# Second block's head projections: pinned high parts, earlier rotary tables, oldest places first

## The chip, the cores and the metric

One core of a Trainium2 chip runs the whole kernel. The metric is device time in microseconds (us) of one execution, median of three runs. TensorE is called PE in the profile, VectorE DVE, ScalarE ACT, GpSimd POOL, SyncE SP. Times of the trace are us from the start of the span.

## The reference

A decoder trunk of one layer over 2048 tokens of width 1024: retention and pooling mixers with one output projection, cross-attention into 256 memory tokens, a gated MLP with a causal convolution, a last norm. The part that the change touches is the combined input projection and what makes its columns into queries, keys, gates and pooled groups:

```
q = rope(q.reshape(B, S, H, Dh), positions)
k = rope(k.reshape(B, S, H, Dh), positions) * (Dh ** -0.5)
...
return jnp.concatenate([t1 * cos - t2 * sin, t2 * cos + t1 * sin], axis=-1)
```

Everything is float32.

## The kernel before, in words

The tokens are worked in two blocks of 1024. A product of two float32 matrices is made of three matmuls on rounded numbers: each operand is split into a high part (rounded, ScalarE) and a low part (what the rounding left, VectorE), and `passes` (lines 268 to 270) runs high by high, high by low and low by high. `split` makes both parts; for weights `Member.high` (L1118) and `low` (L242) do.

The second block's projections stand in `head_projections`. Eight pairs of column tiles (PAIRS) are each computed from seven products of sums of quarters instead of eight plain ones: 56 `items` in all, each of twelve matmuls (4 row tiles, 3 passes). For an item three things are needed.

- Its weight: `fetch` (L1112, SyncE) loads 256 KB from the weights (`w_qkgu`) or from sums of weights that POOL's DMAs made earlier (`Ad`), into one of seven places (`raws`: halves of R, and two of S).
- The weight's high and low part: `fill` takes one of four pairs (`prs`: three in Q, one in another S), calls `high`, and on the next call `low`, which frees the place.
- Its right-hand side, `operand`: sums of quarters of the block's input, split into G and E. `quarter_sums` makes two sets while the values run on TensorE. It leaves two more sums in four slots of Z; `turned_sums` splits them into the values' old place (`split` for the first four tiles, `negated`, L1596, for the others), then Z has room.

`scaled_tables` asks SyncE for the rotary tables (`rope_d`, L1631: four transfers of 64 partitions, 256 KB each, cosine and sine) into the first freed Z slots, and VectorE multiplies them by the row norms. They are needed when a pair of queries or keys is finished (`final`). Both generators are run from `todo`, two `step`s after each item.

The scheduler of the framework may move instructions on an engine; `tc.keep_in_program_order` keeps one where the program has it, `tc.issue_after` puts what is in it behind an instruction. Under the projections POOL goes on making sums of the MLP's weights (`Ud`): a small ScalarE instruction (halo, L1031) starts each burst of DMAs. After the last item the output projection begins: its first weights (L1978, L1991, L1992) are loaded to halves of R and S that the items leave, split by L258. `settle` splits the finished heads (L258, G and E).

Of the kernel before, what the change touches and what calls it, by code (L numbers as in the profile page):

```python
# [11 lines left out]
AF = mybir.ActivationFunctionType  # L12
# [5 lines left out]
KT = D // P  # L18
SEQ = 2048
NMEM = 256  # L20
T = 1024
SUB = 512
# [114 lines left out]
def trunk(ctx, tc, xT, memT, pos, w_qkgu, w_v, wkv, wqT, wo, wout_r, wout_p, poolT, w_up, w_dn, vecs, consts, outT):  # L137
    nc = tc.nc
    pe, act, dve, pool, sp = nc.tensor, nc.scalar, nc.vector, nc.gpsimd, nc.sync
# [17 lines left out]
    def new_s(dtype, at):  # L157
        return cp.tile([P, T], dtype, tag=f"S{at}", name=nm("S"))
# [8 lines left out]
    R = cp.tile([P, 3 * T], F32, tag="R", name="R")  # L167
    Q = cp.tile([P, 3 * T], F32R, tag="Q", name="Q")
    S = [new_s(F32, j) for j in range(2)]
    raws = Places([(R, j * T) for j in range(3)] + [(r, 0) for r in S], T)  # L170
# [70 lines left out]
    def tt(eng, out, a, b, op):  # L241
        return eng.tensor_tensor(out=out, in0=a, in1=b, op=op)  # L242
# [6 lines left out]
    def stt(out, a, s, b, op0=ALU.mult, op1=ALU.add):  # L249
        dve.scalar_tensor_tensor(out=out, in0=a, scalar=s, in1=b, op0=op0, op1=op1)  # L250
# [4 lines left out]
    def split(src, hi, lo, g=None, kept=False):  # L255

        if g is None:
            one = act.activation(hi, src, AF.Copy)  # L258
            tt(dve, lo, src, hi.bitcast(F32), ALU.subtract)
        else:  # L260
            one = act.activation(hi, src, AF.Identity, scale=g)
            stt(lo, src, g, hi.bitcast(F32), ALU.mult, ALU.subtract)
        if kept:
            tc.keep_in_program_order(one)
# [36 lines left out]
    def xpair(k, s):  # L301
        return X[:, 2 * k, s * SUB : (s + 1) * SUB], X[:, 2 * k + 1, s * SUB : (s + 1) * SUB]
# [796 lines left out]
    class Member:  # L1099
# [15 lines left out]
        def high(self, i, pr):  # L1115
            w = self.n * P
            p2 = pr.r.rearrange("p (i n) -> p i n", i=2)
            act.activation(p2[:, 0, :w], self.raw[i].f[:, :w], AF.Copy)  # L1118
            return p2[:, 0, :w], p2[:, 1, :w]
# [436 lines left out]
    def fourth(r, j):  # L1556
        return r.r[:, 2 * j * SUB : (2 * j + 1) * SUB], r.r[:, (2 * j + 1) * SUB : (2 * j + 2) * SUB]

    def part_of(z, i, j):
        at = (j // 2) * 2 * T + i * T + (j % 2) * SUB  # L1560
        return z.f[:, at : at + SUB]

    def quarter_sums(b, t1, t2, z):
# [11 lines left out]
        for j in range(KT // 2):  # L1575
            x11, x12, x21, x22 = ahead.pop(0)
            d3, d4 = part_of(z, 0, j), part_of(z, 1, j)
            g1, g2 = mixg[:, j : j + 1], mixg[:, j + 4 : j + 5]
            r = TT.take()
            t = r.f[:, :SUB]  # L1580
            tc.keep_in_program_order(act.activation(t, x12, AF.Identity, scale=g1))
            tc.keep_in_program_order(tt(dve, x12, x11, x12, ALU.subtract))
            split(x12, *fourth(t1, j), g1)
            yield
            stt(d3, x22, g2, t, ALU.mult, ALU.subtract)
            stt(x11, x11, g1, d3, ALU.mult, ALU.add)
            negated(x11, *fourth(t2, j))
            yield
            stt(d4, x21, g2, x11, ALU.mult, ALU.subtract)
            r.free()  # L1590
            if j + 2 < KT // 2:
                ahead.append(load(j + 2))
            yield

    def negated(src, hi, lo):
        act.activation(hi, src, AF.Copy, scale=-1.0)  # L1596
        stt(lo, src, -1.0, hi.bitcast(F32), ALU.mult, ALU.subtract)

    def head_projections(b, v, rb, t1, t2, z):
# [2 lines left out]
        nonlocal raws, prs  # L1602
        pieces, far = B.arenas[0], new_e(F32)
        more = new_s(F32R, 0)
        raws = Places([(R, j * SUB) for j in range(5)] + [(S[1], j * SUB) for j in range(2)], SUB)
        side = Arena(R, 5 * SUB, 1, SUB).take().f
        prs = Places([(Q, j * T) for j in range(3)] + [(more, 0)], T)
        t3 = pieces.take(4)
        todo, ready, mix, gates, outs, tables = [], [], [None] * KT, {}, {}, []

        def place():
            return Z.take() if Z.room() else far.take()

        def turned_sums():
            for j in range(KT // 2):
                split(part_of(z, 0, j), *fourth(t3, j))
                yield
            z.free(0, 1)
            z.free(2, 1)
            for j in range(KT // 2):  # L1620
                negated(part_of(z, 1, j), *xpair(j, 1))
                yield
            z.free(1, 1)
            z.free(3, 1)

        def scaled_tables():
            out = Z.take(2)
            tables.append(out)
            for to, half in ((0, 0), (0, 1), (2, 0), (1, 1)):
                p, i = slice(64 * half, 64 * half + 64), min(to, 1)  # L1630
                sp.dma_start(out.f[p, i * T : (i + 1) * T].rearrange("p (s c) -> p s c", s=NS), rope_d[to].rearrange("(s p) c -> p s c", s=NS))  # L1631
            yield
            yield
            for i in range(2):
                for s in range(NS):
                    d = out.f[:, i * T + s * SUB : i * T + (s + 1) * SUB]
                    tt(dve, d, d, rb[s].f[:, :SUB], ALU.mult)
                yield
# [37 lines left out]
        class Heads(Member):  # L1676
# [6 lines left out]
            def begun(self):  # L1683
                both_gates = self.groups[0] // 4 == 2
                self.acc = []
                for n in self.groups:
                    if n // 4 == 2:
                        gates[n % 4] = None if both_gates else [TT.take() for _ in range(NS)]
                    if n // 4 == 2 and not both_gates:
                        self.acc.append([g.f[:, :SUB] for g in gates[n % 4]])  # L1690
                    else:
                        r = place()
                        self.acc.append([r.f[:, q * SUB : (q + 1) * SUB] for q in range(NS)])
                        outs[n] = r

            def evac(self, i, ps):
                role, q = ((0, 0), (1, 1), (0, 1), (0, 0), (1, 1), (0, 1), (1, 0))[i]
                d = self.acc[role][q]
                if (role, q) == (1, 0):
                    self.final(role, q, d, ps)  # L1700
                elif (role, q) in self.seen:
                    tt(dve, d, d, ps, ALU.subtract if role else ALU.add)
                    self.final(role, q, d, d)
                else:
                    self.seen.add((role, q))
                    act.activation(d, ps, AF.Copy, scale=-1.0 if role else 1.0)
# [85 lines left out]
        def step():  # L1792
            if todo and next(todo[0], True) is not None:
                todo.pop(0)

        todo += [turned_sums(), scaled_tables()]
        for at, (m, i) in enumerate(items):
            while len(made) <= at or highs:
                fill()
# [3 lines left out]
            pr = made[at].r.rearrange("p (i n) -> p i n", i=2)  # L1803
# [29 lines left out]
        raws = Places([(R, j * T) for j in range(3)] + [(r, 0) for r in S], T)  # L1833
# [72 lines left out]
    todo = folded_weights()  # L1906
# [16 lines left out]
    for b in range(NB):  # L1923
# [19 lines left out]
        else:  # L1943
            t1, t2 = (B.arenas[0].take(4) for _ in range(2))
            v, z = Z.take(4), Z.take(4)
# [11 lines left out]
            finish()  # L1957
            rb = normed[1]
            mix = head_projections(b, v, rb, t1, t2, z)
        for r in rb:  # L1960
            r.free()
# [129 lines left out]
    raws = Places([(R, j * SUB) for j in range(6)] + [(r, j * SUB) for r in S for j in range(2)], SUB)  # L2091
# [114 lines left out]
```

## Time and profile before

| | |
|---|---|
| median of 3 runs | 2466.07 us (2465.82 to 2468.02) |
| profiled execution | 2467.87 us, of it span 2466.1 us |
| PE busy | 2417.9 us, 98% |
| weight loads on PE busy | 2019.7 us, 82% |
| DVE busy | 1726.2 us, 70% |
| ACT busy | 1288.9 us, 52% |
| POOL busy | 316.1 us, 13% |
| mean granted clock of PE | 0.992 |

A row of a timeline reads: start, length, engine, line, operation, output tile <- input tiles, form, and in brackets how long the engine had been idle before it and what ended that. The busy share says little here, since PE is nearly always busy; what a stage may still give shows in PE's pauses and in the granted clock of the stretches around them. The values of the second block end and its head projections begin near 701 us; the output projection follows near 895 us.

### The profile page before, as it was taken

The page shows a single profiled execution, that of the slowest core. Times are in us where ns is not written, and L with a number is a line of the kernel's source. Part 1 is how long each engine was busy: PE and PEld are TensorE (multiplying, and loading weights), DVE is VectorE, ACT ScalarE, POOL GpSimd, SP SyncE. Part 2 cuts the span into 40 slices and gives each one's busy share as a digit, 9 for nine tenths or more (in the row PEclk, how much of TensorE's full clock was granted, in tenths as well). Part 3 has the DMA queues.
Part 4 walks back from the last instruction along what each step waited for, and adds up shares of the span by engine and source line. Part 5 has one row for each costly group of instructions (what it writes and reads, how often), then busy time and mean ns, then how long its engine had stood idle before and what let it go on. Part 6 is the DMA issues. An engine that isn't in the chain of part 4 may idle for free.

```text
span 2466.1 us, 33272 instructions
## 1 busy us (share of the span) xinstructions
PE 2417.9 (98%) x11294; PEld 2019.7 (82%) x11294; DVE 1726.2 (70%) x2917; ACT 1288.9 (52%) x2349; POOL 316.1 (13%) x485
## 2 busy tenths in 40 slices
PE   6999999999989999999999999999999999999997
PEld 6888888888878887878888888888888888888886
DVE  8646576564756665565778776886767698867875
ACT  6333423443435554434655655675555577666663
POOL 1000000054255554200000100020000000000000
PEclk9999999999999999999999999999999999999998
DMA  8133524389899999766568664765556478768951
GB/s 292 45 111 111 160 76 136 124 219 324 250 273 274 260 236 321 197 232 213 171 200 270 208 188 151 234 214 162 160 159 216 132 230 307 246 185 283 344 164 69
DMA packets 263595, 502.35 MB, mean 204 GB/s; under 512 B 28800, under 2 KB 57600, under 8 KB 263424
## 3 DMA queue, kind: packets, MB, share of 16 engines
q1 hardware_dynamic: 201536, 385.90, 47.8%
q0 software_dynamic: 37376, 86.00, 14.9%
q10 hardware_dynamic: 24512, 28.32, 3.3%
q8 instruction: 89, 1.46, 0.2%
q14 instruction: 82, 0.67, 0.1%
HBM read 398.65 MB, written 187.43 MB: 238 GB/s over the span
## 4 chain that ended last, share of the span: by engine, by line
PE 93%; DMA 3%; DVE 3%; issue 1%; ACT 0%; SPq 0%; POOL 0%; POOLq 0%; DVEq 0%; ACTq 0%
PE mm L270 29%; PE mm L268 29%; PE mm L269 29%; DMA T<-Xd 1%; PE aux L808 1%; PE aux L824 1%; PE aux L797 1%; PE aux L268 1%; PE aux L269 1%; PE aux L270 1%; PE aux L826 1%; PE aux L349 1%; DMA Z<-rope_d 1%; DMA T<-xT 0%; DVE T L242 0%
## 5 line engine op out<-in xcount | busy, mean ns | idle before, releaser
L268 PE MATMUL mm<-G,Q 128*128 128x512 f32 (+1 forms) x1745 | 673.4, 386 | 19.8 <-ACT Q L258 11.0
L270 PE MATMUL mm<-G,Q 128*128 128x512 f32 (+1 forms) x1745 | 669.9, 385 | 10.5 <-DVE Q L242 10.4
L269 PE MATMUL mm<-G,Q 128*128 128x512 f32 (+1 forms) x1617 | 621.2, 384 | 0.0
L269 PE MATMUL mm<-G,E 128*128 128x512 f32 x1084 | 421.6, 389 | 0.0
L268 PE MATMUL mm<-G,E 128*128 128x512 f32 x1084 | 420.1, 390 | 0.0
L270 PE MATMUL mm<-G,E 128*128 128x512 f32 x1084 | 419.2, 389 | 0.0
L268 PEld LDWEIGHTS mm<-G,Q 128*128 128x128 f32 x1745 | 332.0, 190 | 84.8 <-ACT Q L258 12.4
L270 PEld LDWEIGHTS mm<-G,Q 128*128 128x128 f32 x1745 | 331.5, 190 | 76.0 <-DVE Q L242 13.2
L269 PEld LDWEIGHTS mm<-G,Q 128*128 128x128 f32 x1617 | 308.0, 191 | 57.1
L242 DVE TENSOR_TENSOR Z<-Z,mm 128x512 f32<-128x512 f32 x296 | 201.4, 681 | 111.7 <-PE mm L270 104.7
L250 DVE SCALAR_TENSOR_TENSOR Z<-Z,vecs 128x1024 f32<-128x1024 f32 x176 | 224.5, 1279 | 50.2 <-ACT Z L1181 45.5
L270 PEld LDWEIGHTS mm<-G,E 128*128 128x128 f32 x1084 | 203.5, 188 | 42.4
L269 PEld LDWEIGHTS mm<-G,E 128*128 128x128 f32 x1084 | 203.5, 188 | 42.2
L268 PEld LDWEIGHTS mm<-G,E 128*128 128x128 f32 x1084 | 203.5, 188 | 42.1 <-ACT Z L1263 0.2
L1118 ACT ACTIVATE E<-R 128x512 fp32r<-128x512 f32 (+1 forms) x165 | 101.5, 615 | 142.3 <-PE mm L269 135.1
L242 DVE TENSOR_TENSOR T<-T 128x512 f32<-128x512 f32 (+3 forms) x220 | 150.5, 688 | 24.3 <-ACT T L411 15.4
L242 DVE TENSOR_TENSOR G<-T,G 128x512 fp32r<-128x512 f32 (+1 forms) x181 | 119.3, 673 | 44.1 <-ACT G L1067 32.8
L242 DVE TENSOR_TENSOR Q<-R,Q 128x512 fp32r<-128x512 f32 x149 | 103.4, 696 | 66.3 <-ACT Q L258 47.1
L1118 ACT ACTIVATE Q<-R 128x512 fp32r<-128x512 f32 (+1 forms) x153 | 94.5, 618 | 85.4 <-PE mm L269 72.2
L1181 ACT ACTIVATE Z<-Z,vecs 128x1024 f32<-128x1024 f32 x88 | 109.1, 1241 | 36.6 <-DVE Z L242 35.6
L1067 ACT ACTIVATE G<-T 128x512 fp32r<-128x512 f32 x157 | 95.7, 624 | 58.1 <-DMA T<-Hd 27.9
L1118 ACT ACTIVATE E<-S 128x512 fp32r<-128x512 f32 (+1 forms) x107 | 65.8, 616 | 105.0 <-PE mm L269 103.4
(338 smaller groups left out, 3776.7 us busy)
## 6 DMA issues: line engine op xcount, KB each, us to landing
T<-Gd SPq DMA_DIRECT2D x168, 256.0 KB, 4.4
Ud<-w_up POOLq DMA_DIRECT2D x132, 256.0 KB, 10.1
Gd<-Z SPq DMA_DIRECT2D x110, 256.0 KB, 2.7
R<-Ud SPq DMA_DIRECT2D x106, 256.0 KB, 2.8
R<-w_up SPq DMA_DIRECT2D x80, 256.0 KB, 3.1
S<-Ud SPq DMA_DIRECT2D x70, 256.0 KB, 2.9
Gd<-T SPq DMA_DIRECT2D x56, 256.0 KB, 3.3
T<-Xd SPq DMA_DIRECT2D x53, 256.0 KB, 4.6
```

Of the source, the lines that this page charges most:

```text
L242: return eng.tensor_tensor(out=out, in0=a, in1=b, op=op)
L250: dve.scalar_tensor_tensor(out=out, in0=a, scalar=s, in1=b, op0=op0, op1=op1)
L268: pe.matmul(ps, lh, rh, start=start, stop=False, skip_group_check=more)
L269: pe.matmul(ps, lh, rl, start=False, stop=False, skip_group_check=more)
L270: latest[0] = pe.matmul(ps, ll, rh, start=False, stop=stop, skip_group_check=more)
L349: pe.matmul(ps[:, t : t + 1], ap, one, start=True, stop=more is None)
L797: pe.matmul(col(sc, c), self.ch(k, c), self.ch(q, c), start=True, stop=True)
L808: pe.matmul(col(self.kv, c), col(self.kn.f, c), self.ch(v, c, h * T), start=True, stop=True)
L824: pe.matmul(col(y, c), col(self.pr.f, c), self.ch(v, c, h * T), start=True, stop=self.cur[c] is None)
L1067: act.activation(hi, x, AF.Copy)
L1118: act.activation(p2[:, 0, :w], self.raw[i].f[:, :w], AF.Copy)
L1181: act.activation(self.c[g].f, a[:, 2:], AF.Identity, bias=cb[:, f : f + 1], scale=cw[2][:, f : f + 1])
```

## The change

Four edits in the second block's head projections.

1. `Heads` gets a `high` of its own, with the activation kept in program order (L1699).
2. `turned_sums` frees two Z slots after its first four splits and goes on with `scaled_tables`, which asks for the tables first and does the other four splits two steps later.
3. `part_of` lays the first sums into the first two Z slots and the second into the last two, so that the first four splits free two slots that lie together.
4. The rooms for weights are listed in the order in which the places before were freed, not R first.

```diff
     def part_of(z, i, j):
-        at = (j // 2) * 2 * T + i * T + (j % 2) * SUB
+        at = i * 2 * T + j * SUB
         return z.f[:, at : at + SUB]
...
-        raws = Places([(R, j * SUB) for j in range(5)] + [(S[1], j * SUB) for j in range(2)], SUB)
+        rooms = [(R, 0), (R, T), (R, 2 * T), None, (S[1], 0)]
+        rooms = [(rooms[i][0], rooms[i][1] + h * SUB) for i in raws.freed for h in range(1 if i == 2 else 2) if i != 3]
+        raws = Places(rooms, SUB)
...
                 split(part_of(z, 0, j), *fourth(t3, j))
                 yield
-            z.free(0, 1)
-            z.free(2, 1)
-            for j in range(KT // 2):
-                negated(part_of(z, 1, j), *xpair(j, 1))
-                yield
-            z.free(1, 1)
-            z.free(3, 1)
+            z.free(0, 2)
+            yield from scaled_tables()
...
             yield
             yield
+            for j in range(KT // 2):
+                negated(part_of(z, 1, j), *xpair(j, 1))
+                yield
+            z.free(2, 2)
             for i in range(2):
...
+            def high(self, i, pr):
+                hi, lo = pr.r[:, :SUB], pr.r[:, SUB:]
+                tc.keep_in_program_order(act.activation(hi, self.raw[i].f, AF.Copy))
+                return hi, lo
...
-        todo += [turned_sums(), scaled_tables()]
+        todo.append(turned_sums())
```

Lines behind the edits move: L1631 becomes L1628, L1706 L1712, L1978 L1984, and L1118 is L1699 for these items.

How it moves instructions shows in the order of each engine's program. On VectorE at the start of the projections, before (Q or S_5484 as output: low parts of weights; G: low parts and negatives of the sums; Z<-Z,T: the tables' scaling):

```order
L242 TENSOR_TENSOR G<-Z_4490,G 128x512
L250 SCALAR_TENSOR_TENSOR G<-Z_4490,G 128x512
L242 TENSOR_TENSOR Q<-R,Q 128x512
L242 TENSOR_TENSOR G<-Z_4490,G 128x512
L242 TENSOR_TENSOR Z_4490<-Z_4490,T 128x512 x4
L242 TENSOR_TENSOR Q<-S_79,Q 128x512
L242 TENSOR_TENSOR Q<-R,Q 128x512
```

And there after the change:

```order
L250 SCALAR_TENSOR_TENSOR G<-Z_4490,G 128x512
L242 TENSOR_TENSOR G<-Z_4490,G 128x512
L242 TENSOR_TENSOR Z_4490<-Z_4490,T 128x512 x2
L242 TENSOR_TENSOR Q<-R,Q 128x512
L242 TENSOR_TENSOR Q<-S_79,Q 128x512 x2
L242 TENSOR_TENSOR S_5484<-R,S_5484 128x512
L242 TENSOR_TENSOR Z_4490<-Z_4490,T 128x512 x2
L242 TENSOR_TENSOR Q<-R,Q 128x512 x2
```

The low parts of the first four items, which stood between the sums and ahead of all the scaling (three of them above the rows shown), went behind its first half. On ScalarE at the same place, before (L1118: high parts of weights; L737: evacuation of the values; L1596 and L258: the sums):

```order
L1118 ACTIVATE Q<-R 128x512
L1596 ACTIVATE G<-Z_4490 128x512
L1031 ACTIVATE halo<-consts 128x2
L258 ACTIVATE G<-Z_4490 128x512
L1596 ACTIVATE G<-Z_4490 128x512
L258 ACTIVATE G<-Z_4490 128x512
L1596 ACTIVATE G<-Z_4490 128x512
L1118 ACTIVATE Q<-R 128x512
L258 ACTIVATE G<-Z_4490 128x512
L737 ACTIVATE Z_4490<-mm_5411,rn_5149 128x4x128
L737 ACTIVATE Z_4490<-mm_5412,rn_5149 128x4x128
```

And after:

```order
L1596 ACTIVATE G<-Z_4490 128x512
L258 ACTIVATE G<-Z_4490 128x512
L737 ACTIVATE Z_4490<-mm_5411,rn_5149 128x4x128
L737 ACTIVATE Z_4490<-mm_5412,rn_5149 128x4x128
L1699 ACTIVATE Q<-R 128x512
L1699 ACTIVATE Q<-S_79 128x512 x2
L1699 ACTIVATE S_5484<-R 128x512
```

The high parts went behind the last two evacuations, and into the order of the items; the third item's (S_5484), which stood far ahead at the place of 691.51 us in the trace, too. SyncE there, before:

```order
L1112 DMA R<-w_qkgu 128x512 x2
L1112 DMA R<-Ad 128x512 x2
L1112 DMA R<-w_qkgu 128x512
L1112 DMA R<-Ad 128x512 x2
L1631 DMA Z_4490<-rope_d 64x2x512 x4
L1112 DMA R<-w_qkgu 128x512
```

And after:

```order
L1112 DMA R<-w_qkgu 128x512
L1112 DMA R<-Ad 128x512 x2
L1112 DMA R<-w_qkgu 128x512
L1628 DMA Z_4490<-rope_d 64x2x512 x4
L1112 DMA R<-w_qkgu 128x512
L1112 DMA S_79<-Ad 128x512 x2
```

The tables moved ahead of two loads of weight sums. Near the end of the projections on ScalarE (G<-E_5483: splits of a finished head; L1706: evacuation of an item), before:

```order
L258 ACTIVATE G<-E_5483 128x512 x4
L1118 ACTIVATE Q<-S_79 128x512
L1706 ACTIVATE Z_4490<-mm_6917 128x512
L258 ACTIVATE G<-Z_4490 128x512 x4
L1118 ACTIVATE S_5484<-S_79 128x512
```

And after:

```order
L1699 ACTIVATE Q<-R 128x512
L258 ACTIVATE G<-E_5483 128x512 x4
L1712 ACTIVATE Z_4490<-mm_6917 128x512
L1699 ACTIVATE Q<-R 128x512
L258 ACTIVATE G<-Z_4490 128x512 x4
```

The high part of the same item moved from behind the four splits to ahead of them.

## The prediction

> **What bounds the kernel now.** I read the page's chain of waits first. It is TensorE work almost throughout, so a change is worth what it does to TensorE's pauses, and only those near the change can move:
>
> ```profile
> PE 93%; DMA 3%; DVE 3%; issue 1%; ACT 0%; SPq 0%; POOL 0%; POOLq 0%; DVEq 0%; ACTq 0%
> ```
>
> Next TensorE's timeline, where the second block's values end and its head projections begin (start, length, form, and in brackets the idle time before, with its releaser):
>
> ```profile
> 701.19 0.39 PE L270 MATMUL mm<-E,G 128*128 128x512 f32 x1
> 704.34 0.68 PE L268 MATMUL mm<-G,Q 128*128 128x512 f32 x1 [2.76 <-ACT Q L1118]
> ...
> 711.08 0.39 PE L269 MATMUL mm<-G,Q 128*128 128x512 f32 x1
> ...
> 714.48 0.39 PE L269 MATMUL mm<-G,Q 128*128 128x512 f32 x1
> 718.90 0.80 PE L270 MATMUL mm<-G,Q 128*128 128x512 f32 x1 [4.03 <-DVE Q L242]
> 719.49 0.63 PE L268 MATMUL mm<-G,Q 128*128 128x512 f32 x1
> ...
> 724.61 0.57 PE L268 MATMUL mm<-G,Q 128*128 128x512 f32 x1
> ```
>
> Two pauses: the first product waits for a high part from ScalarE, the fourth for a low part from VectorE. In full flow a matmul starts every (714.48 − 711.08)/15 = 0.227 us. From 719.49 to 724.61 twelve steps take 0.427 each. The windows (busy us of PE, PEld, DVE, ACT, POOL, then the granted clock and the DMA share) say why:
>
> ```profile
> 701.10:704.50 3.40, 0.64 (x4) 0.21 (x3) 3.40 (x7) 3.40 (x8) 1.98 (x5) 1.00 1.10 218
> 704.50:707.90 3.40, 3.40 (x9) 2.64 (x10) 1.64 (x3) 1.46 (x3) 1.05 (x2) 0.50 1.08 290
> 714.70:718.10 3.40, 0.17 (x1) 0.00 (x0) 2.44 (x4) 0.00 (x0) 1.90 (x3) 1.00 1.09 280
> 718.10:721.50 3.40, 2.60 (x6) 2.14 (x7) 3.37 (x8) 0.63 (x1) 1.91 (x3) 0.51 1.10 265
> 721.50:724.90 3.40, 3.40 (x9) 2.66 (x9) 2.40 (x5) 0.72 (x2) 1.58 (x3) 0.50 1.07 325
> ```
>
> Each pause is followed by half clock. The whole price: without a pause the stage's first matmul would start at 701.19 + 0.23 = 701.42. Between 704.34 and 714.48 there are 38 starts; the 39th, due at 701.42 + 38 × 0.227 = 710.0, comes at 718.90, 8.9 late. Thirteen steps to 724.61 take 5.71 instead of 2.95, another 2.8. **11.6 us** is all that can be won here.
>
> Who causes it is in the chain's pieces and in the timelines of VectorE, ScalarE and SyncE:
>
> ```profile
> 682.93 8.47 DMA R<-w_qkgu
> 696.12 2.62 DMA R<-Ad
> 703.89 0.63 SPq L1631
> 704.57 12.36 DMA Z<-rope_d
> ```
>
> ```profile
> 692.17 0.69 DVE L242 TENSOR_TENSOR S<-R,S 128x512 fp32r<-128x512 f32 x1 [5.87 <-ACT S L1118]
> ...
> 714.83 1.29 DVE L242 TENSOR_TENSOR Z<-Z,T 128x512 f32<-128x512 f32 x2 [8.69 <-DMA Z<-rope_d]
> 716.95 1.29 DVE L242 TENSOR_TENSOR Z<-Z,T 128x512 f32<-128x512 f32 x2 [0.83 <-DMA Z<-rope_d]
> 718.16 0.68 DVE L242 TENSOR_TENSOR Q<-S,Q 128x512 fp32r<-128x512 f32 x1
> ```
>
> ```profile
> 691.51 0.63 ACT L1118 ACTIVATE S<-R 128x512 fp32r<-128x512 f32 x1 [9.38 <-DMA R<-w_qkgu]
> ...
> 699.30 0.62 ACT L1596 ACTIVATE G<-Z 128x512 fp32r<-128x512 f32 x1
> 699.82 0.62 ACT L258 ACTIVATE G<-Z 128x512 fp32r<-128x512 f32 x1
> ...
> 703.65 0.63 ACT L1118 ACTIVATE Q<-R 128x512 fp32r<-128x512 f32 x1
> ```
>
> ScalarE sits 9.38 us in front of a high part whose weight is in flight; by the order it belongs to the third product, while the first product's stands at 703.65. VectorE stops too (5.87). Later VectorE stands 8.69 + 0.83 us before the rotary tables, with the low part of the product that TensorE runs fourth queued behind.
>
> **The change part by part.**
>
> *High parts pinned.* No instruction is added. In the new order the values' evacuations and the sums' splits stand ahead of the first high part, and the four first high parts follow in product order. Their weights: the last of the four is asked where the load of 697.39 (below) stood, behind VectorE's stall of 5.87 that goes, so near 691.5; with 8.47 us (above) it lands by 700, and ScalarE no longer waits for a weight. The last value matmul ends at 701.19 + 0.39 = 701.6; its evacuation costs half of the 1.24 here:
>
> ```profile
> 704.71 1.24 ACT L737 ACTIVATE Z<-mm,rn 128x512 f32<-128x512 f32 x2
> ```
>
> So the first high part starts near 702.2, and as 703.65 led to 704.34, the product starts near **702.9** instead of 704.34.
>
> *Tables asked sooner.* The splits of the sums now need only the values' matmuls of the last tile:
>
> ```profile
> 693.48 0.39 PE L269 MATMUL mm<-G 128*128 128x512 f32 x1
> ```
>
> They begin near 693.9 and step by 699.82 − 699.30 = 0.53; the fourth ends at 696.1, VectorE's partner of it (0.68) at 696.9, and SyncE then asks for the cosine's two halves at about 696.9 and 697.55. The sine's two follow the eighth split, near 699.4. Before, all four were issued in a row, the cosine's second and third:
>
> ```profile
> 702.55 2.66 SPq L1631 DMA_DIRECT2D Z<-rope_d  x4
> 696.90 1.65 POOL L1013 DMA_DIRECT2D Ud<-Ud  x2 [0.77 <-DMA Ud<-Ud]
> ```
>
> On SyncE they now pass two loads of sums for later products, and they meet POOL's burst (second row). What do they take? SyncE's timeline and answers of the DMA view for the single loads issued then (KB each, us to landing):
>
> ```profile
> 697.39 0.33 SPq L1112 DMA_DIRECT2D R<-w_qkgu  x1
> R<-w_qkgu SPq DMA_DIRECT2D x1, 256.0 KB, 6.2
> 700.15 2.12 SPq L1112 DMA_DIRECT2D R<-Ad  x2
> R<-Ad SPq DMA_DIRECT2D x1, 256.0 KB, 7.3
> ```
>
> Each issue stands over its answer (of the two at 700.15, the first). The load at 696.12, just before POOL's burst, took 2.62, the last table load 12.36: those are the ends. I take 7.3, nearer to the loads inside the burst: cosine at 697.55 + 7.3 = 704.9.
>
> The Trainium skill, "DMA: Bandwidth & Descriptors", section "Issuing engines are not separate DMA queues", says that transfers started by SyncE and GpSimd share 16 engines and interleave. By that rule the sooner loads still queue with POOL's; the trace agrees (2.62 us without the burst, 6.2 within).
>
> *A new wait comes with it.* On VectorE the two cosine multiplications now stand **ahead of the low parts of products 0 to 3**; before, all four were ahead of the tables. TensorE has work for four matmuls with high parts alone (to 702.9 + 0.9 = 703.8) and then waits. From the start of two multiplications to TensorE before: 718.90 − 716.95 = 1.95. So the restart is T = 704.9 + 1.95 = **706.9**. The sine comes by 699.4 + 0.65 + 7.3 = 707.4, when VectorE has just done four low parts (48 matmuls, 10.9 us of work): hidden.
>
> The fifth matmul would be due at 701.42 + 4 × 0.227 = 702.3, so the delay is 4.6. The new pause, 3.1 us, lies between the old ones of 2.76 and 4.03; I charge the first one's slow window, eight matmuls by 0.2 = 1.6. **Start: 11.6 − 4.6 − 1.6 = 5.4 won.**
>
> *Places.* The oldest-free rule only lets the first loads go to rooms whose readers finish first; it moves no byte. At the other end the last weights now sit where the output projection's second weight wants to land, so that one is asked some 18 us later than before. Its rows (before's load, then the last low part, whose end now frees the room; the size and latency of such a load; the product's start) are:
>
> ```profile
> 868.44 0.33 SPq L1978 DMA_DIRECT2D R<-wout_r  x1
> 887.17 0.68 DVE L242 TENSOR_TENSOR S<-S,S 128x512 fp32r<-128x512 f32 x1
> R<-wout_r SPq DMA_DIRECT2D x1, 192.0 KB, 6.0
> 895.78 0.39 PE L268 MATMUL mm<-G,Q 128*128 128x512 f32 x1
> ```
>
> On before's clock it lands at 887.85 + 6.0 = 893.9, with its high part (0.63) at 894.5, just ahead of the product: 0 to 2 us late. And a pause there goes, since the high part was queued behind four splits and is now ahead of them:
>
> ```profile
> 882.47 0.50 PE L268 MATMUL mm<-G,Q 128*128 128x512 f32 x1 [1.05 <-ACT Q L1118]
> ```
>
> **End: 1.05 won, 0 to 2 lost; I take 0.5 won.**
>
> *Layout of the sums* swaps slots and costs nothing: the same splits read other columns. *In between* (725 to 880) TensorE has no pause now, and a pinned high part follows the evacuation of the product before: with four pairs it has three products, 8.2 us, before it is needed. I take nothing; the cover gone, it would cost as in the slow rival.
>
> Sum: 5.4 + 0.5 = **5.9 us faster.** The profiled execution took 2467.87 (2466.1 span and 1.8 around it), 1.8 above the median of 2466.07; taking the difference from both, 2462.0 and **2460.2** as the median.
>
> **The rivals.**
>
> *The wait only moves.* The tables take 10 to 12.4 us, as their last load did. T = 697.55 + 10…12.4 + 1.95 = 709.5 to 711.9, delay 7.2 to 9.6, clock 1.6 to 2.8: between 2.8 won and 0.8 lost at the start, with the end about 2464.5. For it: DMA is full (1.10). Against: those rows had three table loads just ahead of them, here there is one.
>
> *The clock stays up.* The chip may judge a whole stretch; two shorter pauses with four matmuls between may not trip it. Then 1.6 more, 2458.6. For it: after the pause of 1.05 the first matmul took 0.50, where those after 2.76 and 4.03 took 0.68 and 0.80. Against: the stretch 701.10 to 704.50 was busy for 0.64 of 3.40 and the clock still fell. The Trainium skill, "TensorE: Matmul & The Clock Gate", Part 1, lets the clock fall to half after an idle window of about 3.4 us that runs freely. By that rule neither new pause would trip it; the trace does not agree as far as a fully idle window is meant, since 2.76 us was enough.
>
> *The tables come at once*, 2.62 us: VectorE's own work holds T at about 703.5, delay 1.2, no slow clock: 10.4 won, about 2455.5.
>
> *Slower: pinned high parts stall the body.* From 725 to 880 a high part can't pass an evacuation any more. If each of some 52 products paused 0.25 us, 13 us would go and 5.9 come: 2473. From 0.11 us each the gain is eaten. Against: 8.2 us of lead. For: no row shows pinned order there.
>
> *It doesn't do what it says:* a pinned high part still waits for a weight, the first product starts at 704.3 as before and the tables come no sooner: 2466. Against: the loads asked by 691.5.
>
> **How the numbers follow.** Chances: forecast (4 to 7.5 won) 0.45, wait only moves 0.22, clock stays 0.12, tables at once 0.06, slower 0.09, no effect 0.06. A measurement of this kernel tells about 0.2%, 4.9 us, from no change. Over that faster: 0.33 of the forecast's 0.45, and 0.18 of the two better ones, 0.51. Same: 0.12 + 0.22 + 0.06 and 0.01 = 0.41. Slower 0.08. The range runs from the tables at once to the moved wait with 2 us lost at the end: 2455.5 to 2468.
>
> **What would show it.** First product near 702.9 with a pause of about 1.3; a second of 2.5 to 3.5 released by VectorE, which waited for the tables; SyncE's table rows at 697 and 699.4; ScalarE without its 9.38; no pause at 882; at 895 none over 1. A restart after 709, or pauses all through 725 to 880, would make the forecast wrong.

## The result, and the profile after

The changed kernel takes **2472.2 us** (median of 13 runs, 2468.07 to 2476.93) against 2467.05 of the kernel before on the same chip (13 runs, 2464.54 to 2470.81). The ratio is 1.0023, with an interval of [1.0015, 1.0032]: slower by 5.2 us, just over the 0.2% that can be told from no change. The prediction said 2460.2, with a range up to 2468.0. The profiled execution took 2476.78 us (span 2474.9, before 2466.1).

The chain of waits of the changed kernel has 2% less of TensorE than before and 1% more of ScalarE:

```profile
PE 91%; DMA 3%; DVE 3%; ACT 1%; issue 1%; POOL 0%; SPq 0%; POOLq 0%; ACTq 0%; DVEq 0%
```

Where the time went shows when TensorE's 11294 instructions are matched by number. Number 3640 starts at 755.18 before and at 749.29 after: 5.89 ahead. Number 4322 stands at 885.11 and 883.69, number 4654 at 955.20 and 965.15. At 700 the profiled run was 1.51 late already. I don't count that to the change: the other kernels measured below are 0.5 to 2.9 late there. So the stages give:

| stage (clock of before) | predicted | measured |
|---|---|---|
| start, 700 to 755 | −5.4 | −7.4 |
| body, 755 to 885 | −1.1 (the pause at 882) | +4.5 |
| end, 885 to 955 | +0.6 | +11.4 |
| all that follows | 0 | −1.1 |

Sum, before rounding: +7.3, with the 1.5 from ahead of 700 the 8.8 by which the two spans differ. The prediction counts the pause of 1.05 at 882.47 to its end; by the clock of before it lies in the body, and it went as forecast (1.4 won from 881 to 885). So the body's 4.5 are 5.8 lost ahead of 881, less 1.4. (The profiled execution is one of the slower ones of the changed kernel, 4.6 above its median.)

TensorE's timeline of the changed kernel, the longer of its pauses in the three stages (the 2.76 and 4.03 at the start and the 1.05 at 882 of before are gone):

```profile
704.38 0.50 PE L268 MATMUL mm<-G,Q 128*128 128x512 f32 x1 [1.29 <-ACT Q L1699]
706.53 0.66 PE L270 MATMUL mm<-G,Q 128*128 128x512 f32 x1 [0.90 <-DVE Q L242]
...
798.32 0.50 PE L270 MATMUL mm<-G,Q 128*128 128x512 f32 x1 [1.14 <-DVE Q L242]
802.09 0.50 PE L268 MATMUL mm<-G,Q 128*128 128x512 f32 x1 [0.40 <-ACT Q L1699]
...
875.60 0.50 PE L268 MATMUL mm<-G,Q 128*128 128x512 f32 x1 [1.37 <-ACT Z L1712]
...
892.91 2.13 PE L849 MATMUL aux<-consts,T 128*128 128x128 f32 x8 [0.68 <-ACT T L844]
...
928.39 0.66 PE L270 MATMUL mm<-G,Q 128*128 128x512 f32 x1 [1.03 <-DVE Q L242]
932.31 1.65 PE L268 MATMUL mm<-E,Q 128*128 128x512 f32 x3 [2.82 <-ACT E L258]
...
949.23 0.79 PE L268 MATMUL mm<-G,Q 128*128 128x512 f32 x1 [2.94 <-ACT Q L258]
```

The pause of 2.82 at 932.31 was there before the change too, but shorter:

```profile
926.99 0.96 PE L268 MATMUL mm<-E,Q 128*128 128x512 f32 x3 [1.27 <-ACT E L258]
```

The windows of the same kernel (as in the prediction: busy us of PE, PEld, DVE, ACT, POOL, the granted clock, the DMA share) show what the clock adds:

```profile
703.60:707.00 3.40, 1.72 (x6) 0.97 (x7) 2.42 (x5) 2.28 (x5) 2.33 (x6) 0.96 1.08 223
707.00:710.40 3.40, 3.40 (x10) 2.69 (x9) 1.28 (x3) 0.00 (x0) 0.95 (x2) 0.54 1.05 289
...
928.60:932.00 3.40, 0.89 (x2) 0.16 (x1) 3.40 (x9) 1.00 (x2) 2.52 (x4) 0.50 1.05 290
932.00:935.40 3.40, 3.09 (x7) 2.42 (x8) 2.71 (x5) 0.89 (x2) 2.75 (x4) 0.50 1.06 373
...
949.00:952.40 3.40, 3.17 (x8) 2.50 (x9) 3.40 (x7) 3.02 (x8) 1.31 (x3) 0.51 1.07 307
```

One slow window at the start, as charged; three at the end, where none was charged.

ScalarE's timeline of the changed kernel shows the two queues that the pinned high parts stand in, or push others into:

```profile
798.96 1.28 ACT L1728 ACTIVATE R<-Z 64x512 f32<-64x512 f32 x2 [2.57 <-DVE Z L242]
800.27 0.63 ACT L1699 ACTIVATE Q<-S 128x512 fp32r<-128x512 f32 x1
...
801.42 0.62 ACT L1699 ACTIVATE Q<-R 128x512 fp32r<-128x512 f32 x1
...
884.74 0.62 ACT L1699 ACTIVATE S<-R 128x512 fp32r<-128x512 f32 x1
890.63 0.63 ACT L258 ACTIVATE Q<-R 128x512 fp32r<-128x512 f32 x1 [5.27 <-DMA R<-wout_r]
...
892.49 2.17 ACT L844 ACTIVATE T<-aux,sm 128x128 f32<-128x128 f32 x8 [1.04 <-DVE sm L246]
```

In the body the high parts at 800.27 and 801.42 stand behind a rotary evacuation (L1728) that waits 2.57 us for VectorE; TensorE has caught up and waits for the second at 802.09. This place is half of what the body loses: 2.9 from 786 to 815 by the clock of before. Another 3.0 go by 881, with the pause of 1.37 at 875.60, which an item's evacuation (L1712) ends; TensorE's own order differs from before there, and what makes this pause was not taken apart. At the end the split of an output-projection weight stands at 890.63 and waits 5.27 for its load, ahead of the scaling of the third head (L844). On VectorE, in a row of the same kernel, the low part of that split waits with it, with the head's root, which L844 needs, queued behind:

```profile
891.29 0.69 DVE L242 TENSOR_TENSOR Q<-R,Q 128x512 fp32r<-128x512 f32 x1 [3.77 <-ACT Q L258]
```

On ScalarE before the change the scaling stood first and ran at 887.14:

```profile
887.14 2.15 ACT L844 ACTIVATE T<-aux,sm 128x128 f32<-128x128 f32 x8
889.13 0.68 ACT L258 ACTIVATE Q<-R 128x512 fp32r<-128x512 f32 x1
```

Another queue of this kind stands further on. There the split of a later weight, which ends TensorE's pause at 949.23, is behind an activation (L411) that waits 3.32 for a load of its own:

```profile
948.02 0.63 ACT L411 ACTIVATE T<-T 128x512 f32<-128x512 f32 x1 [3.32 <-DMA Xd<-T]
948.56 0.61 ACT L258 ACTIVATE Q<-S 128x512 fp32r<-128x512 f32 x1
```

### The profile page after: what moved, and what is told of

Read it like the earlier page. It is cut to its first block, busy times and chain, and to the rows that moved or that the text cites. A ratio compares the mean times of both kernels' runs of the same rounds, so it can differ in the third digit from the quotient of the medians.

```text
span 2474.9 us, 33261 instructions
## 1 busy us (share of the span) xinstructions
PE 2423.6 (98%) x11294; PEld 2020.8 (82%) x11294; DVE 1727.0 (70%) x2917; ACT 1287.8 (52%) x2349; POOL 315.5 (13%) x485
## 4 chain that ended last, share of the span: by engine, by line
PE 91%; DMA 3%; DVE 3%; ACT 1%; issue 1%; POOL 0%; SPq 0%; POOLq 0%; ACTq 0%; DVEq 0%
PE mm L268 29%; PE mm L270 29%; PE mm L269 29%; DVE T L242 1%; DMA T<-Xd 1%; PE aux L349 1%; PE aux L797 1%; PE aux L268 1%; PE aux L269 1%; PE aux L270 1%; DVE Z L242 1%; PE aux L824 1%; PE aux L808 1%; DVE Q L242 0%; DMA Hd<-T 0%
## 5 line engine op out<-in xcount | busy, mean ns | idle before, releaser
L1118 ACT ACTIVATE E<-R 128x512 fp32r<-128x512 f32 (+1 forms) x165 | 101.4, 615 | 145.3 <-PE mm L269 134.1
L1118 ACT ACTIVATE E<-S 128x512 fp32r<-128x512 f32 (+1 forms) x107 | 65.8, 615 | 105.1 <-PE mm L269 103.4
L242 DVE TENSOR_TENSOR E<-R,E 128x512 fp32r<-128x512 f32 (+1 forms) x131 | 87.7, 672 | 43.0 <-ACT E L1118 41.9
```

## The experiments

At first the theory was that pinned order costs what is lost in the body and at the end; the rival, that the oldest places do, because they shift the last weights into the output projection's rooms. All runs in one table, sorted by what is pinned. The stages are the differences of TensorE's starts to before, each from one profiled execution, with that of before the change as the reference; "places" and "tables" say whether edit 4 and edits 2 and 3 are in. Each ratio is to the kernel before on the same chip. The stages of a single execution and the medians part by up to 4 us (e16: 2.8 lost over the three stages, 6.5 by the medians), so a difference of a few us between two rows proves nothing by itself.

| run | pinned pairs | places | tables | median us | ratio, interval | start | body | end |
|---|---|---|---|---|---|---|---|---|
| the change | all 8 | yes | yes | 2472.20 | 1.0023 [1.0015, 1.0032] | −7.4 | +4.5 | +11.4 |
| e2 | all 8 | no | yes | 2473.92 | 1.0030 [1.0019, 1.0042] | −10.2 | +4.5 | +9.0 |
| e4 | all 8 | no | no | 2473.83 | 1.0028 [1.0018, 1.0038] | −7.5 | +3.8 | +9.2 |
| e16 | all 8 | yes | no | 2473.57 | 1.0022 [1.0014, 1.0031] | −7.2 | +3.8 | +6.2 |
| e9 | all 8, splits moved | yes | yes | 2470.12 | 1.0013 [1.0005, 1.0022] | −9.2 | +4.4 | +6.3 |
| e6 | all but the last | yes | yes | 2464.25 | 0.9993 [0.9984, 1.0002] | −5.0 | +4.2 | +1.3 |
| e12 | all but 4th and last | yes | yes | 2465.61 | 0.9995 [0.9986, 1.0003] | −6.8 | +4.0 | +1.9 |
| e13 | all but 5th and last | yes | yes | 2469.07 | 1.0007 [0.9999, 1.0016] | −10.2 | +3.3 | +6.9 |
| e5 | last | yes | yes | 2473.07 | 1.0026 [1.0016, 1.0036] | −5.1 | −0.8 | +13.2 |
| e15 | last | yes | no | 2468.96 | 1.0006 [0.9997, 1.0014] | −10.3 | −0.8 | +14.5 |
| e1 | first | yes | yes | 2459.45 | 0.9964 [0.9952, 0.9976] | −9.1 | +0.3 | +0.8 |
| e8 | first | no | yes | 2459.84 | 0.9973 [0.9963, 0.9982] | −6.1 | +0.3 | +0.4 |
| e7 | first | no | no | 2460.45 | 0.9978 [0.9969, 0.9987] | −8.5 | +0.3 | +0.1 |
| e14 | first | yes | no | 2461.45 | 0.9973 [0.9962, 0.9984] | −6.6 | +0.4 | +0.6 |
| e3 | none | yes | yes | 2462.63 | 0.9980 [0.9971, 0.9988] | −8.6 | 0.0 | +0.9 |
| e10 | none | no | yes | 2467.64 | 1.0006 [0.9997, 1.0015] | −1.8 | 0.0 | +1.1 |
| e11 | none | yes | no | 2457.36 | 0.9962 [0.9949, 0.9974] | −11.8 | 0.0 | +0.5 |

### One part undone, or done alone (e1 to e4)

e1 pins in the first pair alone, e2 lists the places as before, e3 drops the pins, e4 has the pins and nothing else of the change.

```diff
# e1
-                tc.keep_in_program_order(act.activation(hi, self.raw[i].f, AF.Copy))
+                one = act.activation(hi, self.raw[i].f, AF.Copy)
+                if self.groups is PAIRS[0]:
+                    tc.keep_in_program_order(one)
# e2
-        raws = Places(rooms, SUB)
+        raws = Places([(R, j * SUB) for j in range(5)] + [(S[1], j * SUB) for j in range(2)], SUB)
```

> All edits stay, but only the high parts of the first seven items are pinned. The profile of the change shows 7.4 us won at the start, 4.5 lost between 775 and 885 and 11.4 lost between 885 and 955. Theory 'order': pinning all 56 high parts makes the losses (three new pauses in the body, L411 ahead of a weight's split at the end). Then the start's gain stays alone: about 6 to 7 us under before, 2460 to 2461. Rival 'places': the last items sit where the output projection's weights land, those come late and hold up ScalarE; then the end still loses about 8 and the time is 2467 to 2470.

> All edits but the order of the rooms, which is as before (R first). Theory 'order': still slower than before by 3 to 6 us, 2470 to 2473, with L411 ahead of the split and its pause near 949. Rival 'places': the end is as before, the start's gain stays, less some in the body: 2461 to 2464.

> All edits but the pinning. Theory 'order': no loss in the body or at the end; at the start the first high part stands between the sums again, so less of the gain, 0 to 4 us: 2463 to 2467. Rival 'places': the end loses about 8: 2471 to 2475.

> The kernel before with nothing but the pinning of all 56 high parts. Theory 'order': the body and the end lose as in the change, except what L411 costs (its place is as before here): start 2 to 4 won, 6 to 10 lost, 2470 to 2475. Rival 'places': nothing lost, 2463 to 2466.

With pins in the first pair alone the start's gain stays, body and end lose 0.3 and 0.8, and the kernel is 0.36% faster than before. With the old places (e2) the end loses 9.0 all the same, and the median of 2473.92 lies 0.9 above the range given: the places don't cause the loss. The pins alone (e4) lose as much as the whole change, though the start wins 7.5 where 2 to 4 were expected. The rival falls. What the pins are needed for is left open by e3: without any, the start still wins 8.6, where 0 to 4 were expected.

### Which pairs (e5 to e8)

```diff
# e5
+                if self.groups is PAIRS[-1]:
# e6
+                if self.groups is not PAIRS[-1]:
```

e7 is before with the first pair pinned and nothing else; e8 is e1 with the old places.

> All edits, but only the seven high parts of the last pair are pinned. In its order the first splits of the output projection's weights (L258) stand ahead of the last head's scaling (L844), as in the change. Theory 'end': these pins alone make the loss after 885, 6 to 11 us of it, with the pause before L849 near 890 and the one near 930; start as without pins (5 to 8 won), no pauses in the body: 2466 to 2471. Rival 'body': the end is late because the pins of the pairs before made it late; then the end here is that of before and the time 2460 to 2463.

> All edits, the high parts of all pairs but the last pinned. L844 stands ahead of the weights' splits here. Theory 'end': body loses 4 to 5 as in the change (pauses near 798 and 802), the end loses under 3; start wins 7: 2462 to 2466. Rival 'body': the end loses as in the change: 2469 to 2473.

> The kernel before with the pinning of the first seven items' high parts and nothing else: old places, old layout, tables behind the negatives. The pin-only kernel won 8.8 at the start without the sooner tables. If the pins alone make that gain: 2458 to 2461, as with all edits and the first pair pinned. If the sooner tables are needed for it: 2463 to 2466.

> All edits with the first pair pinned, but the old order of the rooms. If the oldest places matter for the start: slower than with them by 1 to 3 us, 2460.5 to 2462.5. If not: 2458 to 2460.

The loss falls apart by place. Pins of the last pair cost 13.2 at the end (6 to 11 were expected) and nothing in the body; pins of the others cost 4.2 in the body and next to nothing at the end. e6 has the same queue in the body as the change; its ScalarE and TensorE rows:

```profile
800.78 1.28 ACT L1730 ACTIVATE R<-Z 64x512 f32<-64x512 f32 x2 [2.57 <-DVE Z L242]
802.08 0.63 ACT L1699 ACTIVATE Q<-S 128x512 fp32r<-128x512 f32 x1
...
887.30 2.15 ACT L844 ACTIVATE T<-aux,sm 128x128 f32<-128x128 f32 x8
889.30 0.68 ACT L258 ACTIVATE Q<-R 128x512 fp32r<-128x512 f32 x1
```

```profile
800.14 0.50 PE L270 MATMUL mm<-G,Q 128*128 128x512 f32 x1 [1.14 <-DVE Q L242]
803.91 0.50 PE L268 MATMUL mm<-G,Q 128*128 128x512 f32 x1 [0.40 <-ACT Q L1699]
```

The body's wait of 2.57 and the pauses of 1.14 and 0.40 are those of the change to the hundredth. At the end the scaling is again ahead of the split. The intervals of e7 and e8 overlap that of e1: under a pinned first pair neither tables nor places can be seen.

### The split, and each remaining edit alone (e9 to e12)

e9 is the change with the first halves of the output projection's weights split behind the third head's scaling (ScalarE's order differs from that of the change in a few rows around 887, but also in later splits up to 949, and TensorE's order behind 890 a little). e10 is the tables edit with the sums' layout alone, e11 the places alone.

```diff
# e9 (scaled_by collects the activations of L844)
-                    split(raw[:, h * SUB : (h + 1) * SUB], pr[:, 0], pr[:, 1])
+                    with tc.issue_after(scaled_by[-9].ins) if h == 0 else nullcontext(): split(raw[:, h * SUB : (h + 1) * SUB], pr[:, 0], pr[:, 1])
# e12
+                if self.groups not in (PAIRS[3], PAIRS[-1]):
```

> All four edits, all high parts pinned; only the splits of the first halves of the output projection's first three weights are issued behind the third head's scaling (L844) on ScalarE. Theory 'one split in the way': after loses 11.4 us between 885 and 955 because L844 starts at 892.5 behind a split whose weight lands at 890.5; with the split behind it, L844 starts within 1 us of 888, the end loses 1 to 4 us as in the run with pins in all pairs but the last (1.5), and the time is 2463 to 2466. Rival 'the weight itself comes late' (asked 4.7 us later than before the change): the end still loses 8 or more and the time stays at 2471 to 2474.

> Before with the tables asked sooner and the sums' layout alone: no pinning, old places. Theory 'places do nothing': as all edits without pinning (2462.6), 2461.5 to 2464, with 5 or more us won at the start. Rival 'the oldest places give part of that gain': 2464.5 to 2467.

> Before with the rooms for weights in the order of freeing alone. Theory 'places do nothing': 2465.5 to 2468.5, within 0.06% of before. Rival 'they start the first loads sooner': 2461 to 2464.

> All four edits, high parts pinned in all pairs but the fourth (its product ends at the pause of 798 to 802) and the last. Theory 'two places in the body': the pinned part behind the rotary evacuation at 799 costs 1.5 of the body's 4.2 us and the clock's answer the rest of that stretch; the pause near 800 goes, the body loses 0 to 2.7 and the time is 2461 to 2463. Rival 'every pinned pair costs its share': the body loses 3.4 or more (5 of 6 pairs), pauses stay near 800, 2463.5 or more.

**e9: less lost, but not for the reason tested.** ScalarE and TensorE of e9 at the end:

```profile
885.50 2.17 ACT L844 ACTIVATE T<-aux,sm 128x128 f32<-128x128 f32 x8 [2.54 <-DVE sm L246]
...
893.60 0.63 ACT L258 ACTIVATE Q<-R 128x512 fp32r<-128x512 f32 x1 [4.66 <-DMA R<-wout_r]
```

```profile
894.28 0.50 PE L268 MATMUL mm<-G,Q 128*128 128x512 f32 x1 [1.76 <-ACT Q L258]
...
928.81 1.65 PE L268 MATMUL mm<-E,Q 128*128 128x512 f32 x3 [3.18 <-ACT E L258]
```

The scaling now runs at 885.50 instead of 892.49, and the end loses 6.3 instead of 11.4. That was expected to be 1 to 4, and the rival of a late weight had 8 or more: neither number came. The difference can't be put down to the scaling. From 885 to 930 e9 loses 7.4, the change 7.7: a weight that lands late now costs a pause of 1.76 at 894.28, and the long one near 930 is still there (3.18, in the change 2.82). The other 4.7 come from 930 to 945. In e9 the later split runs ahead of L411, and the pause at 949.23 is gone.

e16 (below) separates the two. From 881 to 965 ScalarE, VectorE and TensorE have the change's order in it, with the first split ahead of the scaling (890.53 and 892.26); only the later split, with its low part, is ahead of L411:

```profile
945.33 0.62 ACT L258 ACTIVATE Q<-S 128x512 fp32r<-128x512 f32 x1
948.45 0.63 ACT L411 ACTIVATE T<-T 128x512 f32<-128x512 f32 x1 [2.51 <-DMA Xd<-T]
```

Its end loses 6.2. In all seven kernels with the last pair pinned the place of this split goes with the time from 930 to 945: behind L411 (the change, e2, e5, e15) 1.2 to 3.7 are lost, ahead of it (e4, e9, e16) 0.7 to 1.0 won.

**e11 and e10: my expectation was the wrong way round.** The places alone win 11.8 at the start and make the fastest kernel measured here; the tables edit alone can't be told from before. SyncE's timeline of before and of e11 shows how the places do it:

```profile
672.32 0.33 SPq L1112 DMA_DIRECT2D S<-w_qkgu  x1
674.51 0.33 SPq L1112 DMA_DIRECT2D S<-Ad  x1
682.93 10.29 SPq L1112 DMA_DIRECT2D R<-w_qkgu  x2
```

```profile
672.54 11.65 SPq L1112 DMA_DIRECT2D S<-Ad  x4
684.79 1.49 SPq L1112 DMA_DIRECT2D R<-w_qkgu  x2
...
696.96 2.62 SPq L1633 DMA_DIRECT2D Z<-rope_d  x4
```

From 672 to 687 before asks for three weights (the second of the group of 10.29 comes at its end, 693), e11 for six. ScalarE and TensorE of e11 then:

```profile
681.89 1.15 ACT L1118 ACTIVATE Q<-S 128x512 fp32r<-128x512 f32 x2 [2.98 <-DMA S<-Ad]
...
683.42 0.62 ACT L1118 ACTIVATE Q<-R 128x512 fp32r<-128x512 f32 x1
```

```profile
701.65 0.39 PE L270 MATMUL mm<-E,G 128*128 128x512 f32 x1
701.88 0.39 PE L268 MATMUL mm<-G,Q 128*128 128x512 f32 x1
```

The high parts of three products are ready by 684.0, 17.8 us before the first product, so the first product (G,Q at 701.88) follows the last value matmul in 0.23 us. With no weight to wait for ahead of the sums' splits, the tables are asked at 696.96 (702.55 before) without any edit of the tables. There is no pause and no slow window at the start at all.

Beside the places the tables edit seems to do harm (e3 against e11: 0.9980 and 0.9962, with intervals that overlap a little), and SyncE's rows show how. In e3:

```profile
698.84 1.29 SPq L1628 DMA_DIRECT2D Z<-rope_d  x2
704.20 0.35 SPq L1112 DMA_DIRECT2D R<-w_qkgu  x1
705.40 1.23 SPq L1628 DMA_DIRECT2D Z<-rope_d  x2
```

The sine's halves stand behind a weight that gets its place at 704.20; in e11 all four requests stand ahead of that weight. TensorE stops for 2.76 us at 717.41 in e3, behind VectorE's wait of 5.90 for the sine.

**e12 left the wrong pair free.** The first parts in the queue near 800 belong to the fifth pair; the rotary evacuations there are the fourth's. It only shows that leaving the fourth free changes nothing.

### What brings the pause back, and the body again (e13 to e16)

```diff
# e13 (all four edits)
+                if self.groups not in (PAIRS[4], PAIRS[-1]):
# e14, e15 (places alone, and)
+                if self.groups is PAIRS[0]:
+                if self.groups is PAIRS[-1]:
```

e16 is the change without the tables edit and the sums' layout.

> All four edits, high parts pinned in all pairs but the fifth (it is the fifth pair's first parts that stand behind the rotary evacuation at 799) and the last. Theory 'queue behind the evacuation': the pauses near 800 go, the body (775 to 885) loses 0 to 2 us instead of 4.2, time 2459.5 to 2462.5. Rival 'every pinned pair costs its share, or VectorE's full queue there pauses TensorE anyway': the body loses 3.4 or more, 2463.5 or more.

> Before with the oldest places and the high parts pinned in the first pair alone, no change to the tables. Theory 'pinning itself makes the first pause': it puts the first high parts behind the values' evacuations, so the first product waits 1.3 us again; start worth 7 to 9.5 us instead of 11.8, time 2458.5 to 2461. Rival 'the tables edit, not the pins, makes the pauses left at the start': no pause at 700 to 720, 2456 to 2458.4.

> Before with the oldest places and the high parts pinned in the last pair alone, no change to the tables. Theory 'pins in the last pair set the end': start as with the places alone (11 to 12 won), the end (885 to 955) loses 9 to 13, final time 2466 to 2471. Rival 'the end's loss needs the other edits as well': end loses under 5, 2457 to 2463.

> The change without its tables edit and the sums' layout: oldest places and all high parts pinned. Theory 'pins decide': start 6 to 9 won, body 3 to 5 lost, end 8 to 12 lost, 2469 to 2474, like the whole change (2472.2) within 3 us. Rival 'the tables edit spoils it': 2458 to 2466.

e14: pinning alone brings the first pause back, TensorE's rows of it:

```profile
704.97 0.50 PE L268 MATMUL mm<-G,Q 128*128 128x512 f32 x1 [1.30 <-ACT Q L1700]
707.83 0.79 PE L270 MATMUL mm<-G,Q 128*128 128x512 f32 x1 [1.61 <-DVE Q L242]
```

The start wins 6.6, 0.4 less than the range given, and the median of 2461.45 lies 0.45 above its range; the direction and the place are the theory's, and the rival's clean start did not come. e15 puts the end's loss on the last pair's pins by themselves, on a kernel whose start is nearly clean (one pause of 0.97): 14.5, more than expected, with this in ScalarE's queue:

```profile
877.87 0.63 ACT L258 ACTIVATE Q<-R 128x512 fp32r<-128x512 f32 x1 [1.04 <-PE mm L269]
...
885.90 1.15 ACT L258 ACTIVATE Q<-R 128x512 fp32r<-128x512 f32 x2 [7.21 <-DMA R<-wout_r]
...
887.44 2.16 ACT L844 ACTIVATE T<-aux,sm 128x128 f32<-128x128 f32 x8
```

Here three splits stand ahead of the scaling, with a wait of 7.21 for a load. e16 loses like the whole change by the medians: the tables edit plays no part in that loss. Its end lost 6.2, under the 8 to 12 expected; in the profile the difference to the change lies at the later split told under e9.

e13 contradicts the single place in the body. With the fifth pair free the change's two pauses near 800 go, but another high part, whose weight is still in flight, makes one (ScalarE of e13):

```profile
788.50 0.63 ACT L1699 ACTIVATE Q<-S 128x512 fp32r<-128x512 f32 x1 [2.97 <-DMA S<-Ad]
```

TensorE stood 1.33 us at 789.18 for it, and the body lost 3.3, between the two theories (0 to 2, and 3.4 or more). Its end is the exception in the table: TensorE stood 4.93 us at 940.91 for the split of a later weight. So two of the body's queues are seen, but not one place whose removal would save it.

## Why the prediction was wrong, point by point

- **First product near 702.9: right.** It came at 704.38 on a clock 1.51 late, 702.87, with a pause of 1.29 (about 1.3 was said).
- **Tables asked sooner, T = 706.9: right in kind, mis-sized.** The restart came at 706.53 − 1.51 = 705.0, since the cosine took less than the 7.3 taken: VectorE started on it at 704.59 − 1.51 = 703.1, not 704.9. So the second pause was 0.90, where 2.5 to 3.5 were said. With the slow window charged, 7.4 were won, not 5.4; as kernels with the same instructions there win from 5.0 to 10.2 (last section), the nearness of the two is partly chance. The sine came later than taken (VectorE waits 3.04 for it, to 709.8 by the clock of before, where 707.4 was said), but TensorE had work and didn't stop: hidden, as said.
- **Places: "it moves no byte" failed.** Alone they win 11.8 at the start, all of the 11.6 that the prediction had counted as the whole price of the two pauses. The step looked at the far end of the list and passed over the near one: the places of before held the third and fourth weight back to 683 and 693. In the change this gain is hidden in part, since the pins put the high parts behind the values' evacuations again (e11 against e14: 11.8 and 6.6).
- **"In between … I take nothing" failed.** 4.5 were lost by 885, in every kernel with pins in the middle pairs 3.3 to 4.5, in those without at most 0.4. Without the pause won at 882 it is 5.8, as much as the whole gain forecast, and per product 5.8/52 = 0.11 us: just where the slower rival says that the gain is eaten. That rival had the mechanism for half of it (a high part that can't pass an evacuation); the loss stands in a few pauses, not in every product. The 8.2 us of lead didn't hold at a place where VectorE has a pool group's sums to work through, so that the evacuation ahead of the high part waits 2.57.
- **"End: 1.05 won, 0 to 2 lost; I take 0.5 won" is the step that decides.** The 1.05 was won. Behind it 11.4 were lost where 0 to 2 were allowed, and no rival named that. The step priced the late weight for the product that uses it. It did not ask what stands behind that weight's split on ScalarE, nor that the pins move instructions that aren't pinned. Shown: the pins of the last pair cause the loss (e5, e15; not e6). Shown by seven profiles, the closest pair of them the change and e16: where the scheduler then puts a later split behind L411, TensorE pauses for it at 949, some 5 of the change's 11.4. That is what one execution of each shows; the medians of the two agree (1.0023 and 1.0022), so what this queue costs on average stays open. For the other 6 to 7 the cause is open too. The split ahead of the third head's scaling is in six of the seven kernels that lose there, but moving it (e9) won only 0.3 from 885 to 930. Argued only: TensorE's order. In all seven, and in none of the others, the last head's retention matmuls (L808) start some 25 to 34 matmuls later than before; VectorE's sum on the head's state starts at 907.41 in the change and 905.04 in e9, both 908.8 or 908.9 by the clock that before had at 885, against 900.57. No run moved these matmuls back.

The Trainium skill, "PSUM — Partial Sum Buffer", section "Engine vs sequencer instructions", says that ScalarE's queue is strictly first in, first out. The rows agree: L844, and on VectorE the root that it needs, ran only after a split that had waited 5.27 for a load they have nothing to do with.

The body stays open in part: that pins in the middle pairs cost 3.3 to 4.5 is shown by eight kernels, but e13 removed one queue and got another, and no run took the pause at 875.60 apart.

## What to carry to other kernels

An instruction pinned on an in-order engine is priced by what stands ahead of it and by what the scheduler then puts ahead of its neighbours: go through the new order to the end of the pinned stretch and read each wait for a load or another engine as a wait of all that stand behind it. Pin only where a stall is seen (the first pair alone kept the gain), and try first whether an earlier load removes it: the order in which rooms are handed out won by itself no less than pins and table requests together (e11 0.9962, e8 0.9973, with intervals that overlap).

The places alone (2457.36 us, 0.9962 [0.9949, 0.9974]) and all edits with the first pair pinned (2459.45, 0.9964 [0.9952, 0.9976]) beat both kernels; between these two the runs don't decide.

## What the runs showed of the hardware that was not expected

**The same instructions, a start worth 5.0 to 10.2.** Six kernels (the change, e1, e6, e9, e12, e13) have all edits and a pinned first pair, and differ only later. All have the first pause of 1.29 to 1.30. Then the cosine table lands sooner or later:

| kernel | VectorE waits for the table | second pause of TensorE | slow windows of 3.4 us | start |
|---|---|---|---|---|
| e13 | 2.26 | none | 0 | −10.2 |
| e1 | 3.10 | 0.42 | 0 | −9.1 |
| e9 | 3.37 | 0.68 | 0 | −9.2 |
| the change | 3.60 | 0.90 | 1 | −7.4 |
| e12 | 4.21 | 1.51 | 1 | −6.8 |
| e6 | 5.13 | 2.45 | 2 | −5.0 |

With the DMA share at 1.0 to 1.1 in all these windows, 2.9 us in the arrival of a load become 5.2 us of time, since the clock answers too. In the change a window with TensorE busy for 1.72 of 3.40 us was enough.

**A pause of 2.76 brought a slow window at one time and none at another.** Windows of e3, around a pause of 2.76 at 717.41:

```profile
714.00:717.40 3.40, 0.65 (x3) 0.19 (x2) 1.94 (x4) 1.21 (x3) 1.59 (x3) 1.00 1.11 240
717.40:720.80 3.40, 3.38 (x15) 2.81 (x16) 3.37 (x8) 0.73 (x2) 2.10 (x3) 1.00 1.11 289
```

The clock stayed at 1.00, where before's pause of 2.76 at 704.34, with 0.64 busy in its window, was followed by 0.50. The Trainium skill, "TensorE: Matmul & The Clock Gate", Part 1, has the clock fall after an idle window of about 3.4 us that runs freely. That the window runs freely fits: the same pause can be split by it or not. That a whole idle window is needed doesn't fit: the change's clock fell after pauses of 1.29 and 0.90 us with a few matmuls between.
